# Gate and up projections of a two-layer trunk by seven block products of 256 tokens, on activations normalized in place

## The chip, the cores and the metric

The kernel runs on one core of one Trainium2 chip. The metric is the device time of one launch in microseconds (us). A core has five engines with a queue each: TensorE (PE, with its weight loads shown as PEld), VectorE (DVE), ScalarE (ACT), GpSimd (POOL) and SyncE (SP), which here only issues transfers. Each queue takes its instructions in the order in which they stand in it; an instruction at the head that waits for another engine holds up all that stands behind it on its own engine.

## The reference

A decoder of two layers over 512 tokens of 1024 channels, all in float32. Each layer has a mixer and then a gated feed-forward part, both behind an RMS norm and added to the residual `h`. The feed-forward part is the one that matters here:

```python
hn = rms_norm(h, norm_ffn[layer])
g = causal_dwconv3(hn @ w_gate, conv_w) + conv_b      # 1024 -> 2816, width-3 conv along the tokens
up = hn @ w_up                                        # 1024 -> 2816
h = h + (silu(g) * up) @ w_down                       # 2816 -> 1024
```

The RMS norm multiplies every token by `rstd` (one over the root of its mean square) and every channel by a gain.

## The kernel before

Activations lie with channels on the 128 partitions and tokens along the free axis: `h` is eight tiles of 128x512 (k = 0..7). A float32 product is made of three matmuls of a rounded type (`mm3`, L125 to L128): each operand is split into a rounded part "hi" and the remainder "lo", and hi*hi, hi*lo and lo*hi are added in PSUM. For the activations the split is in `hg` (L149): `Norm.add` (L162) writes hi and lo of `h` times the gain. `rstd` is not in them; it is applied to the results (`done`, L460), so that TensorE need not wait for it.

Weights come in chunks of 512 KB into one of four `raw` buffers (L111, issued by SP), ScalarE rounds them to `whi` (L121), VectorE subtracts to `wlo` (L122), both from rings of five buffers (L119, L120).

Gate and up are computed by `gate_up` (L437) for two slices of 128 columns at a time, f = 0, 2, ..., 20. Such a block takes four chunks (gate and up, upper and lower half of the 1024 channels) and makes 4 outputs x 8 k x 3 = 96 matmuls with a moving operand of 512 tokens, in four PSUM banks of the seven in the ring `mm` (L42). `done` then takes each finished bank: for a gate, VectorE multiplies by `rstd` into a padded tile (L465), makes the convolution in three steps (L231 to L233), ScalarE applies silu (L469), GpSimd multiplies by `rstd` again, for the up part (L470); for an up, VectorE multiplies the bank with it (L474) and `split` makes the activation's hi and lo (L221, L223).

The slices go in two halves, `HALVES` (L435): 12 slices of gate and up, the down projection of these 12, then 10 and the down projection of these. In layer 0 the down projection is `project` (L247: weights on the stationary side, result added to `h` at L266). In layer 1 it is a group over eight banks (`group8`, L698) with the activations on the stationary side, whose result is added to `y`, the transposed residual. The transposes (`turn_residual`, L637) stand after blocks f = 2 to 8. In all groups the last `tail` of the k go output by output, so that outputs finish one after the other (`group`, L130).

The order of the work in each queue is set by the tile framework's scheduler when the program is built. Buffers of a ring are used in turn: an instruction that writes one waits for the last reader of what lay in it before.

Of the kernel before, what the change touches and what calls it, by code (L numbers as in the profile page):

```python
# [15 lines left out]
P = 128  # L16
D = 1024
# [13 lines left out]
def tile_trunk(ctx: ExitStack, tc: tile.TileContext, x, norm_mix, norm_ffn, final_norm,  # L31
# [53 lines left out]
    def params(layer, rows_, queue=nc.sync):  # L85
        rows = sum(n for _, _, n in rows_)
        pk = cp.tile([P, P], F32, tag=f"pk{layer}", name=f"pk{layer}")
# [42 lines left out]
    def group(name, outs, ks, lhs, rhs, tail, on_done, before=None):  # L130
# [6 lines left out]
        for i, j in order:  # L137
            if i > at and before is not None:
                before(ks[i])
            at = max(at, i)  # L140
            if j not in banks:
                banks[j] = mm_bank(f"{name}_{j}")
            mm3(banks[j], lhs(ks[i], j), rhs(ks[i], j), i == 0, i == len(ks) - 1)
            if i == len(ks) - 1:
                on_done(j, banks[j])


    h = [cp.tile([P, S], F32, name=f"h{k}") for k in range(NK)]
# [6 lines left out]
    class Norm:  # L155
# [22 lines left out]
        def rstd(self):  # L178
            ps = aux_bank(f"ss_{self.name}")
            hi = tp.tile([P, S], F32R, tag=f"ms{S}", bufs=1, name=f"ssh_{self.name}")  # L180
            lo = tp.tile([P, S], F32R, tag=f"sd{S}", bufs=1, name=f"ssl_{self.name}")
# [14 lines left out]

    def newton(ms, n, name, r):


        sd = tp.tile([P, max(n, LINE)], F32, tag=f"sd{max(n, LINE)}", bufs=1, name=f"sd_{name}")[:, :n]  # L200
# [5 lines left out]
    def inv_sqrt(r, ss, n, name):  # L206

        ms = tp.tile([P, max(n, LINE)], F32, tag=f"ms{max(n, LINE)}", bufs=1, name=f"ms_{name}")[:, :n]
# [226 lines left out]
    HALVES = ((0, 12), (12, 22))  # L435

    def gate_up(layer, prm, rstd, ap, acts, f, tail):  # L437

        cs = slice(f * P, (f + 2) * P)
        ch = {}  # L440
        for half in range(2):
            for key, w in (("g", w_ffn_gate), ("u", w_ffn_up)) if tail < NK else ():
                ch[key, half] = weights(w[layer][half * 512 : (half + 1) * 512, cs]
                                        .rearrange("(k p) c -> p k c", p=P), 4, 256,
                                        f"{key}{layer}_{f}_{half}")
        if tail == NK:
            for key, w in (("g", w_ffn_gate), ("u", w_ffn_up)):
                for half in range(2):
                    ch[key, half] = weights(w[layer][half * 512 : (half + 1) * 512, cs]
                                            .rearrange("(k p) c -> p k c", p=P), 4, 256,  # L450
                                            f"{key}{layer}_{f}_{half}")

        def lhs(k, j):
            hi, lo = ch["gu"[j // 2], k // 4]
            c = slice((j % 2) * P, (j % 2 + 1) * P)
            return hi[:, k % 4, c], lo[:, k % 4, c]

        gates = {}

        def done(j, ps):  # L460
            ft = f + j % 2
            r = rstd()
            if j < 2:
                t = padded_tile()
                nc.vector.tensor_tensor(t[:, 2:], ps, r, ALU.mult)  # L465
                c = ap.tile([P, S], F32, tag="c", bufs=2, name=f"c{layer}_{ft}")
                conv3(c, t, *(prm("cf", i * NF + ft) for i in range(3)))
                s = ap.tile([P, S], F32, tag="s", bufs=3, name=f"s{layer}_{ft}")
                nc.scalar.activation(s, c, AF.Silu, bias=prm("bf", ft))  # L469
                nc.gpsimd.tensor_tensor(s, s, r, ALU.mult)  # L470
                gates[j] = s
            else:
                s = gates[j - 2]
                nc.vector.tensor_tensor(s, ps, s, ALU.mult)  # L474
                acts[ft] = split(ap, s, f"a{layer}_{ft}", tag="a", bufs=12)

        group(f"gu{layer}_{f}", range(4), list(range(NK)), lhs, lambda k, j: hg_k(k), tail, done)

    def lazy_rstd(norm):
        got = []  # L480

        def get():
            if not got:
                got.append(norm.rstd())
            return got[0]

        return get

    def ffn0(norm):
        nonlocal prm1  # L490
        with tc.tile_pool(name="f0", bufs=1) as ap:
            rstd = lazy_rstd(norm)
            nxt = None
            for a, b in HALVES:
                acts = {}
                for f in range(a, b, 2):
                    gate_up(0, prm0, rstd, ap, acts, f, 4 if f == 0 else NK)
# [3 lines left out]
                project(f"d0_{a}", w_ffn_down[0], acts, list(range(a, b)), nxt)  # L501
# [127 lines left out]
    def ffn1(norm):  # L629
        with tc.tile_pool(name="f1", bufs=1) as ap:  # L630
            fin = ap.tile([P, D], F32, name="fin")
            nc.scalar.dma_start(fin, final_norm.rearrange("(o d) -> o d", o=1).to_broadcast([P, D]))
            rstd = lazy_rstd(norm)
# [3 lines left out]
            def turn_residual(t):  # L637
                for half in range(2):
                    ps = mm_bank(f"hT{t}_{half}")
                    for i in range(4):  # L640
                        nc.tensor.transpose(ps[:, i * P : (i + 1) * P],
                                            h[half * 4 + i][:, t * P : (t + 1) * P], ident)
                    nc.scalar.copy(y[t][:, half * 512 : (half + 1) * 512], ps)
# [100 lines left out]
```

## Time and profile before

| | us |
|---|---|
| three runs | 1020.39, 1022.35, 1022.51 |
| median | 1022.35 |
| the profiled execution | 1023.1 |
| its span (first to last instruction) | 1021.4 |
| busy: TensorE | 1009.4 |
| busy: VectorE | 559.0 |
| busy: ScalarE | 345.3 |
| busy: GpSimd | 126.7 |

The page of the profile gives busy times, 40 slices of the span, transfers, the chain of work that ended last, and groups of instructions. A row of a group reads: line, engine, operation, output<-input, shape, xcount | busy us, mean ns of one | idle us of the engine just before them, and what ended it. A row of the timeline reads: start and duration in us, engine, line, operation, output<-input, shape, xcount [idle before <- what ended it]; neighbours that follow one another are merged into one row with their count. A row of the windows reads: stretch, its length, then busy us (and count) of TensorE, its weight loads, VectorE and so on, the granted clock, the share of the DMA engines and GB/s.

### The profile page before, as it was taken

Reading aid. Unit: us, or ns where it says so; the run is one execution under the profiler, and the core shown is the slowest. Engines: PE = TensorE matmul, PEld = TensorE weight load, DVE = VectorE, ACT = ScalarE, POOL = GpSimd, SP = SyncE. Lnnn points to the kernel's source line nnn. Section 1 sums busy time; section 2 is a strip of 40 time slices with the busy share of each in tenths; the row PEclk is TensorE's granted clock in tenths of the full one; section 3 lists DMA queues with packets and bytes.
Section 4 is the critical chain, followed back from the end, with each engine's and each line's share of the span. In section 5 each row is a group of like instructions: output and inputs, shape, how many; then the busy total and the mean of one; then the engine's idle time right before and its main releaser. Section 6 shows DMA issues by size and latency. Waiting matters only on the chain.

```text
span 1021.4 us, 11177 instructions
## 1 busy us (share of the span) xinstructions
PE 1009.4 (99%) x4485; PEld 832.4 (81%) x4485; DVE 559.0 (55%) x706; ACT 345.3 (34%) x449; POOL 126.7 (12%) x113
## 2 busy tenths in 40 slices
PE   9999999999999999999999999999999999999997
PEld 6788888888888888888878888888888888888885
DVE  5997567755623455654423645486554226565526
ACT  5423443323312223333345444433332212332313
POOL 3141121111100011111110001211111001111100
PEclk9999999999999999999999999999999999999999
DMA  7432233332333332332333123324233224233302
GB/s 232 154 103 83 83 103 98 92 115 89 95 111 84 96 109 83 103 104 78 106 126 103 62 91 96 103 83 124 83 103 103 84 81 124 83 104 103 100 3 83
DMA packets 74719, 101.24 MB, mean 99 GB/s; under 512 B 3268, under 2 KB 52652, under 8 KB 74668
## 3 DMA queue, kind: packets, MB, share of 16 engines
q1 hardware_dynamic: 73324, 98.96, 31.2%
q10 hardware_dynamic: 1344, 1.58, 0.5%
q8 instruction: 35, 0.57, 0.2%
q14 instruction: 16, 0.13, 0.0%
HBM read 98.42 MB, written 2.10 MB: 98 GB/s over the span
## 4 chain that ended last, share of the span: by engine, by line
PE 97%; DVE 1%; DMA 1%; issue 0%; POOL 0%; ACT 0%; DVEq 0%; POOLq 0%; ACTq 0%
PE gu L127 16%; PE gu L128 16%; PE gu L126 16%; PE dn L127 4%; PE d L126 4%; PE d L128 4%; PE dn L128 4%; PE d L127 4%; PE dn L126 4%; PE oo L128 1%; PE u L127 1%; PE u L126 1%; PE oo L127 1%; PE u L128 1%; PE oe L127 1%; PE oe L126 1%
## 5 line engine op out<-in xcount | busy, mean ns | idle before, releaser
L126 PE MATMUL gu<-hgh,whi_g 128*128 128x512 f32 x352 | 137.3, 390 | 0.0
L128 PE MATMUL gu<-hgh,wlo_g 128*128 128x512 f32 x352 | 137.0, 389 | 0.0
L128 PE MATMUL gu<-hgh,wlo_u 128*128 128x512 f32 x352 | 137.0, 389 | 0.0
L127 PE MATMUL gu<-hgl,whi_g 128*128 128x512 f32 x352 | 136.9, 389 | 0.0
L126 PE MATMUL gu<-hgh,whi_u 128*128 128x512 f32 x352 | 136.9, 389 | 0.0
L127 PE MATMUL gu<-hgl,whi_u 128*128 128x512 f32 x352 | 136.9, 389 | 0.0
L470 POOL TENSOR_TENSOR s<-s,rstd_f 128x512 f32<-128x512 f32 x44 | 66.5, 1512 | 529.8 <-ACT s L469 529.8
L121 ACT ACTIVATE whi_g<-raw_g 128x1024 fp32r<-128x1024 f32 x44 | 46.6, 1059 | 169.9 <-PE gu L127 107.8
L122 DVE TENSOR_TENSOR wlo_u<-raw_u,whi_u 128x1024 fp32r<-128x1024 f32 x52 | 63.8, 1229 | 59.5 <-ACT whi_u L121 59.1
L122 DVE TENSOR_TENSOR wlo_g<-raw_g,whi_g 128x1024 fp32r<-128x1024 f32 x44 | 54.4, 1236 | 47.3 <-ACT whi_g L121 46.9
L126 PEld LDWEIGHTS gu<-hgh,whi_u 128*128 128x128 f32 x352 | 66.1, 188 | 13.8
L127 PEld LDWEIGHTS gu<-hgl,whi_u 128*128 128x128 f32 x352 | 66.1, 188 | 13.7
L128 PEld LDWEIGHTS gu<-hgh,wlo_g 128*128 128x128 f32 x352 | 66.1, 188 | 13.7
L126 PEld LDWEIGHTS gu<-hgh,whi_g 128*128 128x128 f32 x352 | 66.1, 188 | 13.6
L128 PEld LDWEIGHTS gu<-hgh,wlo_u 128*128 128x128 f32 x352 | 66.1, 188 | 13.6
L127 PEld LDWEIGHTS gu<-hgl,whi_g 128*128 128x128 f32 x352 | 66.1, 188 | 13.6
L121 ACT ACTIVATE whi_u<-raw_u 128x1024 fp32r<-128x1024 f32 x52 | 55.0, 1059 | 58.6 <-PE gu L127 20.7
L126 PE MATMUL d<-a_hi,whi_d 128*128 128x512 f32 x176 | 68.6, 390 | 0.0
L128 PE MATMUL d<-a_hi,wlo_d 128*128 128x512 f32 x176 | 68.5, 389 | 0.0
L127 PE MATMUL d<-a_lo,whi_d 128*128 128x512 f32 x176 | 68.5, 389 | 0.0
L126 PE MATMUL dn<-whi_dn,a_hi 128*128 128x512 f32 x176 | 68.5, 389 | 0.0
L127 PE MATMUL dn<-wlo_dn,a_hi 128*128 128x512 f32 x176 | 68.5, 389 | 0.0
(236 smaller groups left out, 1772.5 us busy)
## 6 DMA issues: line engine op xcount, KB each, us to landing
raw_g<-in_w_ffn_gate_dram SPq DMA_DIRECT2D x44, 512.0 KB
raw_u<-in_w_ffn_up_dram SPq DMA_DIRECT2D x44, 512.0 KB, 3.9
raw_d<-in_w_ffn_down_dram SPq DMA_DIRECT2D x22, 512.0 KB, 3.5
raw_dn<-in_w_ffn_down_dram SPq DMA_DIRECT2D x22, 512.0 KB, 3.3
raw_oe<-in_w_out_even_dram SPq DMA_DIRECT2D x8, 512.0 KB, 3.3
raw_v<-in_w_in_odd_dram SPq DMA_DIRECT2D x8, 512.0 KB, 3.6
raw_u<-in_w_in_odd_dram SPq DMA_DIRECT2D x8, 512.0 KB, 3.5
raw_oo<-in_w_out_odd_dram SPq DMA_DIRECT2D x8, 512.0 KB, 3.3
```

The costliest lines, as they stand in the source:

```text
L121: nc.scalar.activation(hi, raw, AF.Copy)
L122: nc.vector.tensor_tensor(lo, raw, hi.bitcast(F32), ALU.subtract)
L126: nc.tensor.matmul(ps, lhs[0], rhs[0], start=start, stop=False)
L127: nc.tensor.matmul(ps, lhs[0], rhs[1], start=False, stop=False)
L128: nc.tensor.matmul(ps, lhs[1], rhs[0], start=False, stop=stop)
L470: nc.gpsimd.tensor_tensor(s, s, r, ALU.mult)
```

## The change

In both layers the blocks f = 4 to 20 are computed by another scheme. A block's result is a 2x2 arrangement: two column slices by two token halves of 256. With the weights cut into A11 (upper 512 channels, first slice) and so on and the activations into B11 (upper 512 channels, first 256 tokens) and so on, seven products of 512 channels by 256 tokens take the place of eight:

- products 1, 2: A11 and A21 (as they come) with B11 and B21; 4: A22 with B21 less a sum;
- products 3, 5, 6, 7: sums and differences of weight quarters with halves or sums of activations.

Each product is 4 k x 3 = 12 matmuls of 256 columns, 7 x 12 = 84 for a gate and as many for an up. Products that are added share a PSUM bank; the partial results 1, 5 and 6 are copied out by ScalarE (`keep`, a copy out of PSUM) when their bank goes on to another product, and VectorE adds them to later ones.

The sums of the weights are made for each block: GpSimd makes eight of 128x512 (`s12`, `s34`) and the remainder of A11 (twice), ScalarE and VectorE split the sums (`both`), a third ring of three buffers, `sum`, holds them. The sums of the activations are made once in each layer: `normalize` multiplies `h` by gain and `rstd`, forms the differences of the halves on GpSimd and writes them, split, over `hg` and into new tiles. For that, `rstd` is now needed before the matmuls. Blocks f = 0 and f = 2 are computed as before (`direct`), and `normalize` runs within f = 2, one pair of k after the other as TensorE is through with it. With normalized activations the multiplications by `rstd` fall away from f = 4 on.

Beside this: the convolution's first step goes from VectorE to ScalarE; the slices go in four parts, each with its down projection; the transposes in layer 1 stand within f = 0, which there has a tail of 2; the fetch of the final gain stands in the last part, in a `raw` buffer; some buffers share rings.

```diff
-    HALVES = ((0, 12), (12, 22))
+    PARTS = ((0, 6), (6, 12), (12, 18), (18, 22))
+    HALF = S // 2
+    NP = NK // 2
...
+        def gated(self, t, ft):
+            ap, prm, n = self.ap, self.prm, f"{self.layer}_{ft}"
+            c = ap.tile([P, S], F32, tag="c", bufs=2, name=f"c{n}")
+            nc.scalar.activation(c, t[:, 0:S], AF.Copy, scale=prm("cf", ft))
+            for i in (1, 2):
+                nc.vector.scalar_tensor_tensor(c, t[:, i : S + i], prm("cf", i * NF + ft), c,
+                                               op0=ALU.mult, op1=ALU.add)
...
+        def normalize(self, kp):
+            n, r = f"{self.layer}_{kp}", self.rstd()
+            x = self.ap.tile([P, 2, S], F32, tag="sum", bufs=3, name=f"x{n}")
+            for i, k in enumerate((kp, kp + NP)):
+                nc.vector.scalar_tensor_tensor(x[:, i, :], h[k], self.prm("ffn", k), r,
+                                               op0=ALU.mult, op1=ALU.mult)
+            b11, b12 = x[:, 0, :HALF], x[:, 0, HALF:]
+            b21, b22 = x[:, 1, :HALF], x[:, 1, HALF:]
+            t = self.ap.tile([P, 4, HALF], F32, tag="sum", bufs=3, name=f"t{n}")
+            nc.gpsimd.tensor_tensor(t[:, 1, :], b22, b12, ALU.subtract)
+            nc.gpsimd.tensor_tensor(b12, b12, b11, ALU.subtract)
+            nc.gpsimd.tensor_tensor(t[:, 0, :], t[:, 1, :], b11, ALU.add)
+            nc.gpsimd.tensor_tensor(t[:, 2, :], b21, t[:, 0, :], ALU.subtract)
+            def halves(dst, src):
+                nc.scalar.activation(dst[0], src, AF.Copy)
+                nc.vector.tensor_tensor(dst[1], src, dst[0].bitcast(F32), ALU.subtract)
+            halves(hg[kp], x[:, 0, :])
+            self.t23[kp] = self.sums(kp)
+            self.t4[kp] = self.ap.tile([P, 2, HALF], F32R, name=f"t4_{n}")
+            halves(self.t23[kp], t[:, :2, :])
+            halves(hg[kp + NP], x[:, 1, :])
+            halves((self.t4[kp][:, 0, :], self.t4[kp][:, 1, :]), t[:, 2, :])
...
+        def seven(self, f, first):
...
+            def both(src, name):
+                hi = wp.tile([P, 2, 4, P], F32R, tag="whi", bufs=5, name=f"whi_{name}")
+                lo = wp.tile([P, 2, 4, P], F32R, tag="wlo", bufs=5, name=f"wlo_{name}")
+                if src is not None:
+                    nc.scalar.activation(hi, src, AF.Copy)
+                    nc.vector.tensor_tensor(lo, src, hi.bitcast(F32), ALU.subtract)
+                return hi, lo
...
+            pair = both(None, f"a11_{n}")
+            for i, key in enumerate("gu"):
+                a11 = raw[key, 0][:, :, :P]
+                nc.scalar.activation(pair[0][:, i], a11, AF.Copy)
+                nc.gpsimd.tensor_tensor(pair[1][:, i], a11, pair[0][:, i].bitcast(F32),
+                                        ALU.subtract)
+                put(key, 1, pair, i)
+            s12 = {}
+            for key in "gu":
+                r0, r1 = raw[key, 0], raw[key, 1]
+                s = ap.tile([P, 2, 4, P], F32, tag="sum", bufs=3, name=f"s12{key}_{n}")
+                nc.gpsimd.tensor_tensor(s[:, 0], r0[:, :, P:], r1[:, :, P:], ALU.add)
+                nc.gpsimd.tensor_tensor(s[:, 1], s[:, 0], r0[:, :, :P], ALU.subtract)
+                pair = both(s, f"s12{key}_{n}")
+                put(key, 5, pair, 0)
+                put(key, 6, pair, 1)
+                s12[key] = s
+                s = ap.tile([P, 2, 4, P], F32, tag="sum", bufs=3, name=f"s34{key}_{n}")
+                nc.gpsimd.tensor_tensor(s[:, 1], r1[:, :, :P], s12[key][:, 1], ALU.subtract)
+                nc.gpsimd.tensor_tensor(s[:, 0], r0[:, :, :P], r0[:, :, P:], ALU.subtract)
+                pair = both(s, f"s34{key}_{n}")
+                put(key, 7, pair, 0)
+                put(key, 3, pair, 1)
+            for key in "gu":
+                hi, lo = parts(*raws[key, 1])
+                for i, product in enumerate((2, 4)):
+                    c = slice(i * P, (i + 1) * P)
+                    stat[key, product] = hi[:, :, c], lo[:, :, c]
+            BANK = {1: "a", 6: "a", 7: "a", 4: "a", 5: "e", 3: "e", 2: "b"}
...
+            def after(key, product, ps):
+                if product in (1, 6, 5):
+                    keep(key, {1: 0, 6: 1, 5: 2}[product], ps)
+                    return
...
+                    dst = {2: (0, lo), 3: (0, hi), 7: (1, hi)}[product]
+                    nc.vector.tensor_tensor(pad(dst[0])[:, dst[1]], ps, k[:, i, :], ALU.add)
...
+            order = [("g", 1), ("g", 5), ("u", 1), ("g", 6), ("u", 5), ("g", 3), ("u", 6),
+                     ("g", 7), ("u", 3), ("g", 2), ("u", 7), ("g", 4), ("u", 2), ("u", 4)]
...
+        def hidden(self, f, arrival=None, before=None):
+            if f == 0:
+                self.direct(f, arrival or list(range(NK)), 2 if before else 4, before)
+            elif f == 2:
...
+                self.direct(f, PAIRS, 1, ready, lambda: self.normalize(NP - 1))
             else:
+                self.seven(f, f == 4)
```

More of the change, by code (lines that the diff above doesn't have):

```diff
@@ L128, in mm3, with group @@
         nc.tensor.matmul(ps, lhs[1], rhs[0], start=False, stop=stop)
-    def group(name, outs, ks, lhs, rhs, tail, on_done, before=None):
+    def group(name, outs, ks, lhs, rhs, tail, on_done, before=None, at_end=None):
         banks = {}
@@ L479, in lazy_rstd, with ffn_weights @@
[L479 to L487, printed above, removed]
+    PARTS = ((0, 6), (6, 12), (12, 18), (18, 22))
+    HALF = S // 2
+    NP = NK // 2
+    PAIRS = [k for i in range(NP) for k in (i, i + NP)]
+    def ffn_weights(layer, f, order):
+        cs = slice(f * P, (f + 2) * P)
+        return {(key, half): fetch(
+            (w_ffn_gate if key == "g" else w_ffn_up)[layer][half * 512 : (half + 1) * 512, cs]
+            .rearrange("(k p) c -> p k c", p=P), 4, 256, f"{key}{layer}_{f}_{half}")
+            for key, half in order}
```

217 lines of the change are left out of this document (156 added, 61 removed).

## The prediction

> **What bounds the kernel now.** I read the page's busy times and its chain of waits first, then the gate and up groups, then one stretch of them by windows.
>
> ```profile
> span 1021.4 us, 11177 instructions
> PE 1009.4 (99%) x4485; PEld 832.4 (81%) x4485; DVE 559.0 (55%) x706; ACT 345.3 (34%) x449; POOL 126.7 (12%) x113
> ...
> PEclk9999999999999999999999999999999999999999
> ...
> PE 97%; DVE 1%; DMA 1%; issue 0%; POOL 0%; ACT 0%; DVEq 0%; POOLq 0%; ACTq 0%
> ...
> L126 PE MATMUL gu<-hgh,whi_g 128*128 128x512 f32 x352 | 137.3, 390 | 0.0
> ```
>
> TensorE is busy from end to end at full clock, and the chain that ended last is TensorE for 97%. The gate and up group has no idle time before it. Its 390 ns is the life of one pipelined matmul, so I take the pace from a window of five blocks (a block is gate and up for two 128-column slices, 96 matmuls):
>
> ```profile
> 344.20:452.90 108.70, 108.63 (x480) 89.97 (x480) 13.15 (x19) 1.00 0.32 97
> ```
>
> 108.63 / 480 = 0.2263 us for a matmul, 21.7 us for a block. Nothing else ends a wait here, so a block gains only if TensorE gets less to do and nobody makes it wait.
>
> **TensorE's part.** In each layer the change leaves f=0 and f=2 as they are and replaces nine blocks of 96 matmuls over 512 tokens by nine of 7 x 4 x 3 x 2 = 168 over 256 tokens, each with its own weight load. No 256-column matmul is in the trace. Half of 0.2263 is 0.113 us, the lower end. Loads could set the pace; the residual's transposes show them over a short moving operand:
>
> ```profile
> 694.79 1.03 PEld L641 LDWEIGHTS hT<-ident,h 128*128 128x128 f32 x8
> ...
> 695.02 1.04 PE L641 MATMUL hT<-ident,h 128*128 128x128 f32 x8
> L641 PE MATMUL hT<-ident,h 128*128 128x128 f32 x32 | 4.1, 272 | 0.0
> ```
>
> Seven steps in 1.04 - 0.27 us are 0.110 us for a load with 128 columns. A straight line from 0.110 at 128 columns to 0.2263 at 512 gives 0.149 at 256, the upper end. I take 0.120, near the half, because a load in 0.110 fits under it. A block is then 20.2 us (19.0 to 25.0) and the 18 blocks gain 18 x 1.5 = 27 us if nothing waits. One product (12 matmuls) is 1.44 us.
>
> The Trainium skill ("TensorE: Matmul & The Clock Gate", Back-to-back issue gap) has 262 cycles for 256 columns; at its 2.4 GHz that is an estimate of 0.109 us, 18.3 us a block and a gain of 61 us. The trace speaks against it: the same table's 518 cycles make 0.216 us for 512 columns, and the row has 0.2263.
>
> **What must now be prepared.** Before, ScalarE rounds a weight (L121) and VectorE takes the rest (L122), four times a block. Now each block also needs sums of its weight quarters. GpSimd makes them: 8 adds or subtracts and 2 remainders, 10 instructions of 128x512 a block. VectorE takes 6 remainders of 128x1024 instead of 4, and keeps 4 multiply-adds, one 512 multiply, one 256 multiply and 2 activation remainders with both inputs in SBUF. The prices:
>
> ```profile
> L122 DVE TENSOR_TENSOR wlo_g<-raw_g,whi_g 128x1024 fp32r<-128x1024 f32 x44 | 54.4, 1236 | 47.3 <-ACT whi_g L121 46.9
> L121 ACT ACTIVATE whi_g<-raw_g 128x1024 fp32r<-128x1024 f32 x44 | 46.6, 1059 | 169.9 <-PE gu L127 107.8
> L221 ACT ACTIVATE a_hi<-s 128x512 fp32r<-128x512 f32 x44 | 27.8, 631 | 33.6 <-DVE s L474 33.6
> L469 ACT ACTIVATE s<-c,prm 128x512 f32<-128x512 f32 x44 | 31.4, 718 | 70.9 <-DVE c L233 70.9
> L474 DVE TENSOR_TENSOR s<-gu,s 128x512 f32<-128x512 f32 x44 | 30.3, 690 | 44.6 <-PE gu L128 43.3 <-PE prm_ps L94 0.7 <-POOL s L470 0.6
> raw_u<-in_w_ffn_up_dram SPq DMA_DIRECT2D x44, 512.0 KB, 3.9
> ```
>
> Back to back a VectorE instruction costs less than it lasts, and GpSimd's cost depends on VectorE; the timeline shows both:
>
> ```profile
> 57.19 0.69 DVE L372 TENSOR_TENSOR zs<-zs 128x521 f32<-128x521 f32 x1
> 57.80 0.70 DVE L372 TENSOR_TENSOR zs<-z 128x527 f32<-128x527 f32 x1
> 170.14 1.29 DVE L465 TENSOR_TENSOR rows<-gu,rstd_f 128x512 f32<-128x512 f32 x2
> 172.13 1.41 DVE L232 SCALAR_TENSOR_TENSOR c<-rows,prm,c 128x512 f32<-128x512 f32 x2
> 173.46 1.41 DVE L233 SCALAR_TENSOR_TENSOR c<-rows,prm,c 128x512 f32<-128x512 f32 x2
> 174.78 1.22 DVE L122 TENSOR_TENSOR wlo_g<-raw_g,whi_g 128x1024 fp32r<-128x1024 f32 x1
> 175.92 0.69 DVE L465 TENSOR_TENSOR rows<-gu,rstd_f 128x512 f32<-128x512 f32 x1
> ```
> ```profile
> 188.09 1.29 POOL L470 TENSOR_TENSOR s<-s,rstd_f 128x512 f32<-128x512 f32 x1 [3.95 <-ACT s L469]
> ...
> 223.65 1.72 POOL L470 TENSOR_TENSOR s<-s,rstd_f 128x512 f32<-128x512 f32 x1 [14.63 <-ACT s L469]
> ...
> 222.99 1.22 DVE L122 TENSOR_TENSOR wlo_g<-raw_g,whi_g 128x1024 fp32r<-128x1024 f32 x1 [0.85 <-ACT whi_g L121]
> ```
> ```profile
> 54.91 5.97 POOL L400 TENSOR_TENSOR ac<-ac,rstd_m 128x512 f32<-128x512 f32 x1 [0.51 <-DVE ac L399]
> ...
> 27.41 0.74 DVE L344 SCALAR_TENSOR_TENSOR hgl<-h,prmmix,hgh 128x512 fp32r<-128x512 f32 x1
> ...
> 32.40 1.47 POOL L175 TENSOR_TENSOR ssq_m<-ssq_m,sq_m 128x512 f32<-128x512 f32 x1 [3.10 <-ACT sq_m L174]
> ...
> 32.64 1.78 DVE L344 SCALAR_TENSOR_TENSOR hgl<-h,prmmix,hgh 128x512 fp32r<-128x512 f32 x1
> ```
>
> VectorE steps 0.61 us for a 512 two-input instruction, 0.67 for a multiply-add, 1.14 for a 1024 remainder. A GpSimd instruction takes 1.29 us alone (I take 1.25 in a row); started under a VectorE remainder it ends 225.37 - 224.21 = 1.16 us after that one does, so the two did not run side by side. The last fence shows the same from both sides: VectorE's 0.74 became 1.78 behind GpSimd, and a GpSimd instruction among VectorE's lasted 5.97. So VectorE's 6 x 1.14 + 4 x 0.67 + 0.61 + 0.35 + 2 x 0.61 = 11.7 us and GpSimd's 10 x 1.04 to 1.25 us exclude each other: 22 to 24 us a block against TensorE's 20.2.
>
> The Trainium skill ("SBUF — State Buffer", Who interferes with whom) says of a VectorE instruction with two SBUF inputs and a reading GpSimd one that the second to issue "fully blocks" until the first finishes; it speaks against this change. The rows agree but for a tail of some 0.1 to 0.2 us.
>
> **Where the wait comes.** There are four raw weight buffers, and a block fills all four. The second gate buffer is freed only when its remainder is taken (products 2 and 4), for which a whi/wlo pair must come free after the third product. Only then is the next block's second half fetched, and GpSimd's queue starts each block with a sum that needs it. In block 1 after a down projection (time from its first matmul, its own sums made during the projection):
> - third product ends 3 x 1.44 = 4.3; ScalarE 1.06, VectorE 1.23, handoffs: 6.8; fetch 3.9: GpSimd starts block 2's sums at 10.9.
> - Ten instructions: four alone, 5.0. Then VectorE's remainder of the first sum and what stands behind it (1024 remainders 3 x 1.14, multiply-adds 4 x 0.67, a 512 multiply 0.61: 6.7 us) against six of GpSimd (6.2 to 7.5). 12.5 if nothing collides, 19.2 if everything alternates; I take 16, the middle. Ends 26.9.
> - ScalarE's queue holds the rounding of the last sum (1.06), an activation's (0.63) and only then the copy of block 2's first product out of PSUM (0.4), for which its fourth product waits: 29.0. VectorE's queue has a like wait: that first remainder stands ahead of the evictions that block 1's last product needs, some 2 us, which lie before 29.0 and add nothing. Eleven products, 15.8: block 2 ends at 44.8 (20.2 x 2 = 40.3 without waits, 43.4 before).
> - From the end of the sums to the next start: those 2.1, the gate's silu 0.72, a copy 0.4, rounding 1.06, remainder 1.23, fetch 3.9: 9.4. Block 3's sums run 36.3 to 52.3, its fourth product starts at 54.4, it ends at 70.2 (65.2 before).
>
> Layer 1's down projection keeps its last four whi/wlo pairs to its last matmul (before too, but there nothing was behind them), so four roundings and remainders start only at the block's start; the second gate buffer comes free at about 10.5 instead of 6.8. All is 3.7 later: 48.5 and 73.9. Per layer stand f=6..10 and 12..16 as threes and 18, 20 as a two: layer 0: 2 x 5.0 + 1.4, layer 1: 2 x 8.7 + 5.1; sum **+34 us**. With 12.5 for the ten it is about 0, with 19.2 about +66.
>
> **Block f=4 and the normalization in place.** It needs all of the new activations, made from rstd on. VectorE has the first rstd result at 170.14 (the L465 row above), and f=2 runs right behind f=0:
>
> ```profile
> 170.19 0.39 PE L126 MATMUL gu<-hgh,whi_g 128*128 128x512 f32 x1
> ```
>
> so TensorE is through f=2 at 191.9. Until the second product's weights (behind nearly all of the normalization in VectorE's queue), VectorE has 4 evictions, 12 multiply-adds, 13 remainders of 512, 4 of 256, 2 multiplies, 1 remainder of 1024: 22.1 us (a 256 one at 0.35, half of 0.61 and a little), of which 18.5 exclude GpSimd's 16 half-size subtractions and adds (0.55 each, estimated as half of 1.04 and a little) and four full ones, 13 us. 170.1 + 31.5 to 35.1 is 202 to 205; I take 203.5, where TensorE, with 1.9 us of other products to do, has waited 10. Then 4 multiply-adds, 3 remainders and two multiplies that wait for GpSimd's last (eight in a row, 10 to 15.6 us together) stand ahead of the fifth product's weights at 216.5: 9 more. 19 - 1.5 = +17.5 in layer 0, and about 3 more in layer 1, where f=0's shorter tail and the transposes moved into it bring rstd later against f=2: **+38 us** (+5 if the two engines overlap fully, +50 at the upper prices).
>
> **At nothing** I cost the same weights fetched (31% of the DMA engines' time), more residual adds of the four parts (VectorE at 0.69, under 33 us of matmuls), the conv's first product moved to ScalarE, and the moved transposes (still 32), the final gain's fetch moved down ScalarE's queue; if the cover of the last part's four slices is gone, about 2 us.
>
> The profiled execution took 1023.1 us for its span of 1021.4; 1023.1 + 34 + 38 = 1095, and as the median of the three runs is 0.8 lower, **1094**.
>
> **Rivals.**
> - Faster: the sums keep ahead and TensorE stays the bound, also through f=4: 1023 - 27 = 996 (962 by the skill's 0.109). Place: the ten GpSimd instructions of a block; block 2's fourth product is due at 20.2 + 4.3 = 24.5, so the ten must take less than 24.5 - 10.9 - 2.1 = 11.5 us, below ten rows of 1.25 and no collision, and needs f=4 covered too. Against it: the 1.72 and 1.78 rows. Chance 0.16.
> - Only f=4 stalls, the later blocks run at TensorE's pace: 1023 - 27 + 41 (waits of 19 and 22) = 1037. The buffers would have to reach further ahead than four do. 0.18.
> - Loads pace the short matmuls at 0.149: 18 x 3.3 = 59 us, partly under the same waits, with f=4: about 1120. Against it: the 0.110 row. 0.06.
> - The change doesn't do what it says: the built program has 168 matmuls of 256 in each of the 18 blocks; nothing is left of this.
> - The forecast: 0.58; the rest, 0.02, near no change.
>
> **Numbers.** Likeliest 1094. The range runs from the f=4 case to the upper prices of the sums: 1033 to 1135; it leaves out the faster case. A difference under 0.2% cannot be told from none here. Faster 0.16, within 0.2% 0.02, slower 0.82.
>
> **What would show it.** Right: GpSimd's instructions at 512 lengthened well over 1.29; TensorE idle before the fourth product of blocks 2 and 3 (released by ScalarE's copy) and before the weights of f=4's second and fifth products; 256-column matmuls 0.12 us apart. Wrong: TensorE back to back through f=6 to 20, or GpSimd at 1.29 throughout.

## The result and the profile after

| | before | after |
|---|---|---|
| median, us (four runs each) | 1022.43 | 1113.91 |
| the profiled execution, us | 1023.1 | 1117.5 |
| its span, us | 1021.4 | 1115.5 |
| busy: TensorE, VectorE, ScalarE, GpSimd | 1009.4, 559.0, 345.3, 126.7 | 1017.4, 699.4, 484.6, 368.5 |

The ratio is 1.0902, with a 95% interval of 1.0866 to 1.0937: 91.5 us slower. The forecast was 1094, 20 us less. The page of the changed kernel, the lines that answer to those shown of before:

```profile
span 1115.5 us, 14532 instructions
...
PE 1017.4 (91%) x5781; PEld 897.8 (80%) x5781; DVE 699.4 (63%) x868; ACT 484.6 (43%) x723; POOL 368.5 (33%) x289
...
PE   8999999499889988998999999975998899889987
...
PEclk9999999599999998999999999996999999999999
...
PE 8%; DVE 4%; issue 2%; POOL 1%; ACT 1%; DMA 1%; DVEq 0%; POOLq 0%; ACTq 0%
```

TensorE is no longer at nine tenths throughout, and its granted clock, which was full in every slice before, has a 5 and a 6 (the two f=4 stages). The chain of waits could be followed back through only about a sixth of the span, where it was 97% TensorE before, so the stages have to be read one by one. The windows of the changed kernel over the eight stretches of seven products (f=4, then six blocks as two threes, then two; layer 0, then layer 1):

```profile
191.95:238.15 46.20, 27.71 (x170) 26.06 (x169) 36.75 (x43) 22.47 (x34) 22.85 (x18) 0.70 0.22 70
270.82:344.32 73.50, 64.47 (x506) 63.66 (x504) 49.30 (x60) 37.81 (x59) 30.45 (x20) 0.95 0.28 87
376.99:448.83 71.84, 65.35 (x505) 64.74 (x504) 49.04 (x60) 37.61 (x59) 30.38 (x20) 0.93 0.30 89
481.50:528.33 46.83, 42.32 (x338) 41.91 (x337) 31.22 (x39) 24.61 (x38) 15.21 (x10) 0.96 0.29 92
742.76:792.47 49.71, 29.16 (x170) 26.62 (x169) 40.10 (x43) 24.22 (x37) 27.03 (x21) 0.73 0.21 64
825.21:898.61 73.40, 63.23 (x505) 62.19 (x504) 53.02 (x62) 38.58 (x61) 34.02 (x22) 0.98 0.32 94
931.26:1006.66 75.40, 64.70 (x505) 63.65 (x505) 53.08 (x61) 38.73 (x61) 34.00 (x22) 0.95 0.31 92
1039.40:1086.29 46.89, 42.52 (x337) 41.87 (x336) 35.02 (x40) 25.51 (x40) 18.74 (x12) 0.96 0.29 90
```

They add up to 483.8 us; the same 18 blocks took 18 x 96 x 0.2263 = 391.0 before. The 92.8 us between them are nearly all of the 94.4 that lie between the two profiled executions: all other stages together moved by 1.6. At 20.16 us of arithmetic a block, more than half of f=4 and a sixth of the rest is something else. What ended TensorE's waits:

```profile
PE ua L616 <- DVE keptu L652: 25.4, 10, 3.7
PE ga L616 <- ACT keptg L627: 20.5, 13, 2.3
PE ga L616 <- ACT hgh L535: 13.8, 4, 5.3
PE ge L616 <- ACT whi_s12g L566: 11.9, 2, 8.5
PE gb L616 <- ACT whi_g L121: 7.6, 2, 4.9
...
PE ue L616 <- ACT whi_s12u L566: 1.0, 1, 1.0
```

The first two rows are the later blocks: the last product of an up waits for VectorE to empty the bank of the one before, and the gate's product 6 (fourth in the order) waits for ScalarE's copy. The others are f=4: the normalized activations (`hgh`), then the sums for product 5 of the gate (second in the order), then product 2's weights (tenth); the sums for product 5 of the up (fifth) hardly count.

### The profile page after: what moved, and what is told of

Its sections match the earlier page's. It is cut to its first block, busy times and chain, and to the rows that moved or that the text cites. A ratio compares the mean times of both kernels' runs of the same rounds, so it can differ in the third digit from the quotient of the medians.

```text
span 1115.5 us, 14532 instructions
## 1 busy us (share of the span) xinstructions
PE 1017.4 (91%) x5781; PEld 897.8 (80%) x5781; DVE 699.4 (63%) x868; ACT 484.6 (43%) x723; POOL 368.5 (33%) x289
## 5 line engine op out<-in xcount | busy, mean ns | idle before, releaser
L584 POOL TENSOR_TENSOR s12g<-raw_g,raw_g 128x512 f32<-128x512 f32 x18 | 26.9, 1496 | 294.2 <-DMA raw_g<-in_w_ffn_gate_dram 275.6
L481 DVE SCALAR_TENSOR_TENSOR c<-rows,prm,c 128x512 f32<-128x512 f32 x88 | 87.2, 1000 | 14.3 <-ACT c L479 14.3
L128 PE MATMUL dn<-whi_dn,a_lo 128*128 128x512 f32 x176 | 68.1, 389 | 0.0
L567 DVE TENSOR_TENSOR wlo_s12g<-s12g,whi_s12g 128x1024 fp32r<-128x1024 f32 x18 | 25.1, 1392 | 51.6 <-ACT whi_s12g L566 51.6
L616 PE MATMUL ua<-t,whi_u 128*128 128x256 f32 x144 | 29.9, 306 | 25.4 <-DVE keptu L652 25.4
L479 ACT ACTIVATE c<-rows,prm 128x512 f32<-128x512 f32 x44 | 31.5, 721 | 44.5 <-DVE rows L647 38.4
L616 PEld LDWEIGHTS ua<-t,whi_u 128*128 128x128 f32 x144 | 24.1, 206 | 27.5 <-DVE keptu L652 27.5
L230 ACT ACTIVATE a_hi<-s 128x512 fp32r<-128x512 f32 x44 | 27.8, 631 | 42.3 <-DVE s L655 19.1
L591 POOL TENSOR_TENSOR s34u<-raw_u,s12u 128x512 f32<-128x512 f32 x18 | 27.4, 1522 | 50.6 <-DVE wlo_s12g L567 49.8
L275 DVE TENSOR_TENSOR h<-d,h 128x512 f32<-128x512 f32 x32 | 21.9, 688 | 34.9 <-PE d L128 34.9
L567 DVE TENSOR_TENSOR wlo_s34g<-s34g,whi_s34g 128x1024 fp32r<-128x1024 f32 x18 | 35.7, 1983 | 10.8 <-ACT whi_s34g L566 10.8
```

The lines of the kernel that those rows point to most:

```text
L128: nc.tensor.matmul(ps, lhs[1], rhs[0], start=False, stop=stop)
L230: nc.scalar.activation(hi, src, AF.Copy, scale=scale)
L479: nc.scalar.activation(c, t[:, 0:S], AF.Copy, scale=prm("cf", ft))
L481: nc.vector.scalar_tensor_tensor(c, t[:, i : S + i], prm("cf", i * NF + ft), c, op0=ALU.mult, op1=ALU.add)
L567: nc.vector.tensor_tensor(lo, src, hi.bitcast(F32), ALU.subtract)
L584: nc.gpsimd.tensor_tensor(s[:, 0], r0[:, :, P:], r1[:, :, P:], ALU.add)
```

## Experiments

All ratios are to the kernel before, run on the same chip beside each experiment. The theory: the weights' sums come too late, because GpSimd's sums and VectorE's work exclude each other and because the fetch of a chunk waits for a remainder; in f=4 the normalization is serial. "Exclude each other" means here that an instruction of the one holds up an instruction of the other until it is done (for short, the exclusion). Rivals: the evictions' order in the queues; the loads; later, the clock.

### The sums left out

```diff
-            pair = both(None, f"a11_{n}")
...
+            ch = {key: parts(*r) for key, r in raws.items()}
+            for key in "gu":
+                for half in range(2):
+                    hi, lo = ch[key, half]
+                    for c, ps_ in enumerate(((1, 5, 6, 7), (2, 3, 4))[half]):
+                        cs_ = slice(c % 2 * P, (c % 2 + 1) * P)
+                        stat[key, ps_] = hi[:, :, cs_], lo[:, :, cs_]
```

> Left out: the weight sums. All seven products keep their form, but take their weights from the four raw chunks of a block, rounded and split as in the kernel before (4 roundings on ScalarE, 4 remainders on VectorE, nothing on GpSimd), so the output is not the reference's. Theory (the sums' preparation makes TensorE wait in the blocks from f=6 on, the normalization in f=4): the 16 later blocks run at 168 x 0.120 = 20.2 us, three in a row 60.5 us instead of 72 to 75; f=4 keeps the wait for the normalization but loses the wait for its fifth product's sums; 1022.4 - 16 x 1.5 + 2 x 20 = 1038, range 1025 to 1055. Rival (the evictions of twice as many half-size products, in queue order, make the waits whoever prepares the weights): three in a row stay at 70 or more, 1095 or more.

Measured: 1023.56, ratio 1.0014 (1.0003 to 1.0025). Windows of this run, f=4 and three later blocks of layer 0:

```profile
192.19:225.39 33.20, 25.20 (x169) 23.96 (x168) 28.45 (x38) 19.63 (x31) 12.23 (x10) 0.85 0.25 81
258.06:318.53 60.47, 60.47 (x505) 60.47 (x504) 34.33 (x53) 29.70 (x48) 0.00 (x0) 1.00 0.31 97
```

TensorE is busy for all 60.47 us: 20.16 a block, 0.120 a matmul, with all evictions of the seven products in place. So neither weight loads nor evictions make the later blocks wait; making and splitting the sums does. What the scheme could gain there, 16 x 1.56 = 25 us, is spent again in f=4 (33.2 and 36.0 us instead of 21.7), which the normalization alone holds up. The rival "evictions" falls.

### Sums that nobody reads

```diff
             ch = {key: parts(*r) for key, r in raws.items()}
+            for key in "gu":
...
+                nc.gpsimd.tensor_tensor(s[:, 0], r0[:, :, P:], r1[:, :, P:], ALU.add)
...
```
(held against the run without sums; the other nine instructions follow)

> As the run without sums, but GpSimd makes ten instructions of 128x512 a block again (sums of the raw chunks), whose results nothing reads; they hold back only the raw buffers. Theory (GpSimd and VectorE exclude each other): VectorE's two-input instructions take up to twice as long beside them and come late, though no matmul depends on a sum: VectorE's 9.4 us of such work and GpSimd's 10.4 to 12.5 make 20 to 22 us a block against 20.2, so a part of the waits comes back, 10 to 30 us over the run without sums. Rival (only the chain sum, rounding, remainder, buffer makes it late): within 5 us of the run without sums, VectorE's durations as in that run.

Measured: 1052.47, ratio 1.0286 (1.0261 to 1.0311): 29 us over the run without sums. A group of VectorE, then the windows of f=4, of three blocks in layer 0 and of three in layer 1:

```profile
L122 DVE TENSOR_TENSOR wlo_g<-raw_g,whi_g 128x1024 fp32r<-128x1024 f32 x44 | 63.4, 1441 | 34.7 <-ACT whi_g L121 34.5
```
```profile
192.09:233.45 41.36, 28.61 (x169) 26.93 (x168) 34.38 (x38) 19.30 (x31) 27.38 (x20) 0.79 0.23 78
266.12:326.59 60.47, 60.47 (x505) 60.47 (x504) 37.14 (x53) 29.48 (x48) 24.75 (x17) 1.00 0.32 97
784.57:849.09 64.52, 60.98 (x505) 60.57 (x504) 46.27 (x55) 29.85 (x50) 31.50 (x20) 1.00 0.35 107
```

The exclusion is there: the remainder's mean goes from 1220 ns without the sums to 1441. The size came out as expected, the place did not: in layer 0's later blocks TensorE still never waits. The 29 us are 18 in f=4 and 11 in the later blocks of layer 1. Whether they arise there because the unread sums lengthen VectorE's instructions, or because they hold the raw buffers, this run does not separate. Layer 0's later blocks show that longer VectorE instructions by themselves cost nothing while they have slack; there it takes the chain through the sums as well.

### The sums on VectorE

```diff
-                nc.gpsimd.tensor_tensor(s[:, 0], r0[:, :, P:], r1[:, :, P:], ALU.add)
+                nc.vector.tensor_tensor(s[:, 0], r0[:, :, P:], r1[:, :, P:], ALU.add)
```
(and so the other three lines of `s12` and `s34`)

> The changed kernel with the eight sums of a block on VectorE instead of GpSimd (the two remainders on GpSimd stay). Theory (exclusion): a sum costs the shared time 0.61 instead of 1.04 to 1.25 us, the two engines together 19 to 20 us a block on VectorE and 2.5 on GpSimd instead of 23 to 25; the period of the later blocks falls from 26.2 to 21 to 23 us; 1114 - 35 = about 1080, range 1060 to 1095. Rival (VectorE's queue, whose evictions come too late, is what counts): 4.9 us more work in that queue, and its first sum waits there for a fetch with evictions behind it; slower than 1114, 1120 to 1150.

Measured: 1054.81, ratio 1.0322 (1.0306 to 1.0339): 59 us less than the changed kernel, for moving eight instructions a block onto the busier engine. Two groups of the changed kernel, then the same two of this run:

```profile
L481 DVE SCALAR_TENSOR_TENSOR c<-rows,prm,c 128x512 f32<-128x512 f32 x88 | 87.2, 1000 | 14.3 <-ACT c L479 14.3
L567 DVE TENSOR_TENSOR wlo_s34g<-s34g,whi_s34g 128x1024 fp32r<-128x1024 f32 x18 | 35.7, 1983 | 10.8 <-ACT whi_s34g L566 10.8
```
```profile
L481 DVE SCALAR_TENSOR_TENSOR c<-rows,prm,c 128x512 f32<-128x512 f32 x88 | 65.5, 757 | 3.4 <-ACT c L479 3.4
L567 DVE TENSOR_TENSOR wlo_s34g<-s34g,whi_s34g 128x1024 fp32r<-128x1024 f32 x18 | 22.0, 1220 | 6.7 <-ACT whi_s34g L566 6.7
```

The same instructions on the same data: 1983 ns beside GpSimd, 1220 without it. Three later blocks take 63.3 us instead of 73.5, f=4 41.0 and 45.1. The theory's direction holds, and it undersold it; "VectorE's queue is too long" falls. The run takes away two things at once, the exclusion and the 1.29 us that a sum lasts on GpSimd even alone; their shares were not told apart here.

### f=4 direct, the normalization a block later

```diff
             elif f == 2:
+                self.direct(f, list(range(NK)), 4)
+            elif f == 4:
...
-                self.seven(f, f == 4)
+                self.seven(f, False)
```
(the last quarter of the normalization goes beside the down projection)

> The changed kernel with the block f=4 as 96 matmuls of 512 columns too, and the normalization in place one block later, its last quarter beside the down projection that follows; seven products only from f=6 on. Theory (the block f=4 with its half-clock stretches costs 24.5 us in layer 0 and 28 in layer 1 over the 21.7 of a direct block): 1114 - 52 = 1062, and up to 10 us more where the last quarter holds back the projection's weights: 1060 to 1075. Rival (the normalization is serial work of VectorE and GpSimd that TensorE waits for wherever it stands): the wait moves to the down projection, 1095 or more.

Measured: 1082.47, ratio 1.0590 (1.0568 to 1.0611): 31 us less, not 52. Windows of f=4 and of the projection behind it, layer 0:

```profile
191.50:213.13 21.63, 21.63 (x96) 17.71 (x95) 15.13 (x21) 8.60 (x14) 7.93 (x9) 1.00 0.15 50
213.13:257.07 43.94, 36.06 (x146) 28.74 (x144) 26.02 (x31) 16.15 (x22) 18.37 (x14) 0.92 0.28 84
```

f=4 is back at its 21.6, and the projection takes 43.9 where it took 32.7: the rival was right to a good part. The normalization now stands ahead of f=4's own evictions in VectorE's queue, and TensorE waits 7.8 us for those and for the activations; the rest is its clock of 0.92.

### Every block direct

```diff
+            elif f < NF:
+                self.direct(f, list(range(NK)), 4)
             elif f == 2:
```

> The changed kernel with every block as 96 matmuls of 512 columns, no normalization in place and no seven products: what is left of the change are the four parts instead of two halves, the residual's transposes inside f=0, the convolution's first product on ScalarE, the later final gain and the smaller buffers. Theory (these cost nothing): 1022 to 1025. Rival (more residual adds, shorter projections and the last part's four slices cost something of their own): 1028 or more, and the later stages would have to be charged less.

Measured: 1025.29, ratio 1.0039 (1.0024 to 1.0054), 3.6 us more than before, at the edge of what the theory gave. Most of it is the last part, whose projection of 96 matmuls takes 23.6 and 23.3 us instead of 21.7, where TensorE waits 1.0 and 1.2 us for the last activations. In the changed kernel the same projection follows a block of seven products and takes 21.9 and 21.7. So the other edits cost the changed kernel next to nothing.

### Matmuls in the waits

```diff
+            def fill(m):
+                if m:
+                    ps = aux_bank(f"fill{n}")
+                    for i in range(m):
+                        nc.tensor.matmul(ps, ones_r, hg[0][0], start=i == 0, stop=i == m - 1)
```
(called ahead of the waiting products)

> The changed kernel with matmuls whose result nobody reads put in front of the products that wait (8 of 512 columns, 1.8 us, before the fourth product and the last product of the later blocks; 4.5 to 8.2 us at the waits of f=4), so that TensorE is busy instead of idle. After the waits the granted clock was 0.5 for stretches of 3.4 to 17 us, where 268 of the short matmuls came 0.22 us apart instead of 0.12: 27 us. Theory A (that is lost time): with the waits filled the clock stays and the time falls by 15 to 27 us, 1087 to 1099. Theory B (the sums and the normalization set when the next wait ends, and a slower TensorE only idles less): within 6 us of 1114 in the later blocks, a few us in f=4; 1105 to 1117.

Measured: 1142.99, ratio 1.1193 (1.1170 to 1.1216): outside both. The stretches of half clock became fewer (44 us of them instead of 89, without those at the kernel's start and end), yet it is 29 us slower. The scheduler, which sees the extra matmuls, had changed the order of ScalarE's queue. The copy stands behind the rounding of an activation (`a_hi`), which waits for VectorE, in both kernels; here the rounding of the last sum (`whi_s34u`) and a silu stand between the two, where the changed kernel has that rounding ahead of `a_hi`, within time in which ScalarE is free anyway, and the silu behind the copy (its rows are shown further down):

```profile
304.67 0.63 ACT L230 ACTIVATE a_hi<-s 128x512 fp32r<-128x512 f32 x1 [3.93 <-DVE s L665]
305.20 1.04 ACT L568 ACTIVATE whi_s34u<-s34u 128x1024 fp32r<-128x1024 f32 x1
306.15 0.70 ACT L486 ACTIVATE s<-c,prm 128x512 f32<-128x512 f32 x1
306.76 0.35 ACT L637 COPY keptg<-ga 128x256 f32<-128x256 f32 x1
```

The rounding of block 2's first sum starts at 291.60 here, so its copy comes 15.2 us later; in the changed kernel it is 286.74 and 300.29, 13.6. The queue changed, and the filling matmuls take time themselves, so this run tells nothing about what the clock costs.

### Five raw buffers

```diff
-        raw = wp.tile([P, a, b], F32, tag="raw", bufs=4, name=f"raw_{name}")
+        raw = wp.tile([P, a, b], F32, tag="raw", bufs=5, name=f"raw_{name}")
```

> The changed kernel with five raw weight buffers instead of four, so that the second gate chunk of the next block no longer waits for the second gate remainder of this one. Theory A (the chain remainder, fetch, sums sets the period of 26.2 us of the later blocks, as the forecast had it): the sums start some us earlier, the period falls to 22 to 24; ten such blocks make 20 to 40 us, 1075 to 1095. Theory B (GpSimd and VectorE excluding each other sets it, whenever the sums start): the period stays at 25 to 26.2, 1105 to 1116.

Measured: 1081.86, ratio 1.0591 (1.0567 to 1.0615), 32 us less, theory A. The first sum of block 2 starts 5.9 us ahead of block 1's first matmul instead of 10.85 us behind it, though GpSimd is as slow as before. Three blocks of layer 0 take 63.8 and 65.2 us, of layer 1 68.1 and 67.3. So the late start and the slow sums are two causes: in the later blocks of the profiles (387.9 us) the fifth buffer takes away 38 us, the sums on VectorE 52, and both together, below, 61. Either one hides most of the other.

This run also prices the clock. Windows of two like waits of 2.6 us for product 6, each with the 3.3 us behind it:

```profile
316.80:319.20 2.40, 0.23 (x2) 0.03 (x1) 2.40 (x4) 1.87 (x4) 0.41 (x1) 1.00 0.25 57
319.40:322.70 3.30, 3.30 (x28) 3.30 (x29) 3.30 (x6) 2.91 (x5) 0.00 (x0) 1.00 0.25 97
413.20:415.60 2.40, 0.20 (x2) 0.00 (x0) 2.40 (x4) 1.91 (x4) 0.36 (x1) 1.00 0.31 67
415.80:419.00 3.20, 3.20 (x21) 3.20 (x22) 3.20 (x6) 2.81 (x5) 0.00 (x0) 0.72 0.23 90
```

After the first the clock stays, after the second it drops to a mean of 0.72. The three blocks around them have waits of 3.2 and 3.0 us and differ by 1.4 us. From this one pair, an estimate: a stretch of 3.4 us at half clock costs about 1.4 where TensorE is the bound. The Trainium skill ("TensorE: Matmul & The Clock Gate", Part 1: The HAM clock gate) has the clock fall after an idle window of some 3.4 us, the windows running freely. The length of the slow stretches, 3.4 us or multiples, agrees; that a wait of 2.6 us is enough, once and not the other time, does not fit a wholly idle window.

### The normalization's sums on VectorE

```diff
-            nc.gpsimd.tensor_tensor(t[:, 1, :], b22, b12, ALU.subtract)
+            nc.vector.tensor_tensor(t[:, 1, :], b22, b12, ALU.subtract)
```
(and so the other three; the weights' sums stay on GpSimd)

> The changed kernel with the 16 half-size sums of the normalization in place on VectorE instead of GpSimd; the weights' sums stay on GpSimd. It is about f=4 alone (46.2 us in layer 0 and 49.7 in layer 1). Theory (as the forecast had it, VectorE's and GpSimd's work there add up because they exclude each other): 22.1 + 16 x 0.35 = 27.7 us ahead of the second product's weights instead of 31.5 to 35.1, so f=4 ends 4 to 7 us earlier in each layer: 1100 to 1106. Rival (the two run side by side and VectorE's own queue sets it): 5.6 us more in that queue, 1114 to 1125.

Measured: 1105.55, ratio 1.0816 (1.0791 to 1.0841), 8 us less. The two f=4 stages, to be held against 46.20 and 49.71:

```profile
192.36:233.68 41.32, 28.20 (x170) 26.74 (x169) 34.99 (x47) 22.18 (x34) 16.09 (x10) 0.71 0.24 78
737.66:781.83 44.17, 25.73 (x169) 24.03 (x168) 38.91 (x53) 23.13 (x36) 17.00 (x10) 0.73 0.24 72
```

4.9 and 5.5 us earlier, in the 4 to 7 that adding up the two engines' work gave: they do add up there.

### The activations' splits behind the next block's copies

```diff
-                        self.act(f, sl[0])
+                        self.late.append((f, sl[0]))
...
+                if i == 1 and self.late:
+                    with tc.issue_after(self.copied.ins):
+                        split_late()
```

> The changed kernel; only ScalarE's queue is changed around the wait for its copy: the roundings and remainders of a block's two activations (0.63 and 0.61 us each) are queued behind the copies of the next block's first two gate products instead of ahead of them. In the profile the copy of block 2's first product stood behind such a rounding, which waited for VectorE, and ended 2.1 us later than ScalarE was free after the last sum's rounding. Theory A (that place in the queue sets the sixth product's wait of 1.1 to 2.6 us, 13 times): 15 to 25 us less, 1089 to 1099. Theory B (the chain of fetch, slow sums and remainders sets the period, and the next wait grows by what this one loses): 1105 or more.

Measured: 1114.92, ratio 1.0916 (1.0899 to 1.0932): no change, theory B. Its waits:

```profile
PE ua L616 <- DVE keptu L652: 39.2, 10, 6.0
...
PE ga L616 <- ACT keptg L627: 4.1, 4, 1.1
```

The wait for the copy fell from 20.5 to 4.1 us, and the wait for VectorE's eviction rose from 25.4 to 39.2. Which instruction ends the wait is settled by the order in a queue; how long a block takes is not.

### Versions without the causes

The first had the sums and the normalization on VectorE, f=4 direct, half of the normalization beside it and half beside the projection.

> Sums of the weights and of the normalization on VectorE; f=4 as 96 matmuls of 512 columns, two quarters of the normalization in place beside it and two beside the down projection that follows, one in each half of its matmuls. Theory (the normalization costs only where TensorE has nothing else; exclusion is gone): the later blocks as with the sums on VectorE (63.2, 63.4, 42.3 and 62.5, 62.1, 41.8 us), f=4 21.7, the projection at most 5 us over 32.4: 1022.4 - 12.3 + 2 x 3 = 1016, range 1010 to 1026. Rival (the normalization is serial work that holds back evictions wherever it is put, as the 11.3 us in the projection with f=4 direct): 1030 or more.

Measured: 1019.95, ratio 0.9985 (0.9976 to 0.9995), as the theory had it. In layer 0 the last quarter of its normalization was made from a residual to which the projection had already added, so it computes something else there; its time is that of the layout. Three blocks took 63.4 and the projections behind f=4 34.8 and 39.9 us. The next version makes that quarter ahead of the residual add, and has five raw buffers:

```diff
+        def behind_f4(self, gi, k):
+            if gi == 0 and k == 1:
+                self.normalize(2)
+            if gi == 0 and k == 3:
+                with tc.issue_after(split_last[0].ins):
+                    self.normalize(3)
```

> Meant as a version that beats both kernels: sums of weights and normalization on VectorE, f=4 direct, two quarters of the normalization beside it and two beside the down projection (the last one behind f=4's activations in VectorE's queue, and ahead of the residual add that changes its input), five raw buffers. Theory (with five buffers the sums no longer wait for the fetch, and VectorE's 20 us a block fit under TensorE's 20.2): three blocks 61 to 62 us instead of 62.5 to 63.2, the projections after f=4 37 to 40: 1010, range 1004 to 1016. Rival (VectorE's own work sets 21 us a block whatever is fetched): as with four buffers, 1017 to 1023.

Measured: 1010.52, ratio 0.9897 (0.9882 to 0.9912): 1% faster than before. Three blocks take 61.4 us in layer 0 and 61.9 and 61.6 in layer 1, with 60.5 the arithmetic; VectorE's own work is no bound at 21 us, and the rival falls. The last one adds the late splits:

> The version with five raw buffers and all sums on VectorE, and the activations' splits queued behind the next block's first copies. Theory (ScalarE's copies and VectorE's evictions are what TensorE still waits for): 2 to 6 us below the version without this. Rival (VectorE is full): within 1.5 us of it.

Measured: 1009.79, ratio 0.9890 (0.9873 to 0.9906), within 1.5 us of it: the 2 to 6 us that were expected did not come. The time is the rival's, though its reason (VectorE is full) does not fit the 61.4 us of the run before. Its page, and its windows of the projection behind f=4 and of three blocks, layer 0:

```profile
span 1008.0 us, 14127 instructions
...
PE 989.4 (98%) x5637; PEld 867.6 (86%) x5637; DVE 741.2 (74%) x1014; ACT 470.1 (47%) x701; POOL 132.3 (13%) x113
...
PEclk9999999999999999999999999999999999999999
```
```profile
214.14:248.71 34.57, 33.39 (x146) 26.75 (x145) 30.25 (x42) 12.11 (x17) 7.42 (x4) 1.00 0.35 105
248.71:310.10 61.39, 60.73 (x506) 60.52 (x504) 53.74 (x74) 37.30 (x59) 6.66 (x4) 1.00 0.34 104
```

With TensorE kept busy the clock stays full, but for 3.4 us in the projection behind f=4 of layer 1 (there 0.96 in the mean), around the end of a wait of 4.3 us. The 16 blocks of seven products bring about 21 of the 25 us that they can; the projections behind f=4 give back 8 (1.9 and 6.4).

## Why the prediction was right, and by what it was short

The sum was +72 us and 92.8 were measured in the blocks it speaks of. Split as TensorE sees them:

| us | forecast | measured |
|---|---|---|
| arithmetic of 18 blocks | -27 | -28 (20.16 a block) |
| waits in f=4, two layers | 19 + 22 | 21.4 + 24.3 |
| waits in the later blocks | 58 (34 + 16 x 1.5) | 49.3 |
| matmuls at half clock | 0 | 26.2 |

(Waits are what gaps of over 0.3 us between the starts of matmuls have over 0.120; the last row is what spacings of 0.14 to 0.3 us have over it.)

- **The matmul of 256 columns** at 0.120 us was right to the digit, and the run without sums shows it unhindered over 60.47 us.
- **The chain of the later blocks** was right in its steps, but for its last link and for layer 1. The timeline of the changed kernel, block 1's first matmul being at 270.82:

```profile
281.67 1.29 POOL L584 TENSOR_TENSOR s12g<-raw_g,raw_g 128x512 f32<-128x512 f32 x1 [21.54 <-DMA raw_g<-in_w_ffn_gate_dram]
...
287.91 2.29 POOL L591 TENSOR_TENSOR s34g<-raw_g,s12g 128x512 f32<-128x512 f32 x1
...
293.58 2.31 DVE L567 TENSOR_TENSOR wlo_s34g<-s34g,whi_s34g 128x1024 fp32r<-128x1024 f32 x1
...
294.77 2.27 POOL L592 TENSOR_TENSOR s34u<-raw_u 128x512 f32<-128x512 f32 x1
...
297.07 1.06 ACT L566 ACTIVATE whi_s34u<-s34u 128x1024 fp32r<-128x1024 f32 x1 [1.25 <-POOL s34u L592]
299.75 0.63 ACT L230 ACTIVATE a_hi<-s 128x512 fp32r<-128x512 f32 x1 [1.62 <-DVE s L655]
300.29 0.35 ACT L627 COPY keptg<-ga 128x256 f32<-128x256 f32 x1
```
```profile
300.69 0.47 PE L616 MATMUL ga<-t23h,whi_s12g 128*128 128x256 f32 x1 [2.32 <-ACT keptg L627]
```

  GpSimd starts at 10.85 (forecast 10.9), its ten instructions take 15.4 (16; that was the middle of 12.5 and 19.2 and not worked out, so this hit is in part luck), block 2's fourth product starts at 29.9 (29.0). From the end of the sums to the end of the copy it is 3.6 us instead of 2.1: the activation's rounding ahead of the copy waits 1.6 us for VectorE, whose queue is behind by its own lengthened remainders. Block 3's sums run from 37.0 to 52.4 (36.3 to 52.3), its fourth product starts at 56.1 (54.4) and it ends at 73.5 (70.2). For layer 1 the forecast had all of this 3.7 us later, with the first sum at 14.6. It comes at 12.1:

```profile
837.30 1.30 POOL L584 TENSOR_TENSOR s12g<-raw_g,raw_g 128x512 f32<-128x512 f32 x1 [7.86 <-DMA raw_g<-in_w_ffn_gate_dram]
```

  Layer 1's later blocks took 195.7 us in all (196.3 forecast) and layer 0's 192.2 (185.2): the match of layer 1 is luck. Its start is later by about 1 us and not by 3.7, which makes up for what is short there as in layer 0. GpSimd's 2.29 and VectorE's 2.31, where each is alone at 1.29 and 1.22, are the exclusion seen from both sides. Sums and raw buffers were tried apart, and each is a cause. Where the chain was cut (sums on VectorE, or a fifth buffer) the time went; where only the place of a wait was moved, it stayed.
- **"A like wait in VectorE's queue adds nothing"** was right too: it is the largest row of the waits, but it lies ahead of the next block's later wait, and the run with late splits shows the two trading places at equal time.
- **f=4**: the waits were right within 5 us in all, and that the two engines' work adds up in it was shown apart (4.9 and 5.5 us). Their places were right in part: in layer 0 the second product's weights came at 206.1 (203.5 forecast). But by the table of waits, 13.8 us in the two layers ended with the normalized activations and 7.6 with product 2's weights, and only 1.0 with the fifth product's; the forecast named neither of the first two as what ends a wait.
- **What failed** is that TensorE's matmuls were priced at full clock throughout. The step "f=4 ... is +38 us" was 14.5 us short with 10 us of slow matmuls in it; the later blocks' +34 was 6 short, with 9 us less waiting and 16 us of slow matmuls. Part of these matmuls only fill what would have been waited otherwise: layer 0's second three has more of them than the first (4.2 against 3.4 us), less waiting (7.2 against 9.7) and ends sooner. So 26 us is what they took, not what a steady clock would bring back; how much that is, was not settled.
- The Trainium skill's "fully blocks" ("SBUF — State Buffer", Summary: rules for kernel authors), held against this change in the forecast, is borne out by these rows and by 1983 against 1220 ns. The run with unread sums adds that blocked instructions with slack cost nothing, in layer 0's later blocks.
- The rivals: loads at 0.149 and evictions are excluded by the run without sums. "Only f=4 stalls" is what a fifth buffer nearly makes of it in layer 0 (63.8 and 65.2 us for three blocks of 60.5). The faster case fails at its condition: the ten instructions took 15.4 us, where it needed less than 11.5.

## What to carry to other kernels

When work is taken from the bound engine and handed to two others, price the two together if they exclude each other, and against the start that buffers allow them. Here a sum that the slower engine makes in 1.29 us was dearer than the same sum in 0.61 on the busier one. A wait that names one instruction is only where a chain surfaces: cut the chain (an earlier fetch, a cheaper link), for moving the waiting instruction moves the wait. And where TensorE will wait some 2.5 us or more again and again, add something for the matmuls behind each wait: here some 1.4 us for a slow stretch of 3.4, by one pair of blocks.

## Of the hardware, not expected

After waits of TensorE of some 2 to 9 us the granted clock was 0.5 for stretches of 3.4 us or a few times that (17 us in one piece in each f=4), 89 us in all; short matmuls then came 0.20 to 0.24 us apart instead of 0.120. Not each such wait was followed by one. And an instruction of VectorE beside GpSimd's sums lasted up to 2.31 us instead of 1.22, while ScalarE's roundings (1.06) and TensorE's matmuls kept their times.
